# A margin on attention matmuls in the planner's list, and ten instead of nine feed-forward groups beside attention

## The chip, the cores and the metric

One core of a Trainium2 chip runs the whole program. The metric is the device time of one execution in microseconds (us). Five engines work side by side: TensorE (PE, with its weight loads as PEld), VectorE (DVE), ScalarE (ACT), GpSimd (POOL) and SyncE (SP), which here issues the DMAs. Each engine runs its own list of instructions strictly in order, so an instruction that waits holds up all that stand behind it on that engine.

## The reference, cut to what matters

Two layers over a residual stream x of 1024 tokens x 1024 features, everything in float32:

```python
for layer in range(2):
    h = rms_norm(x, mix_norm_g)
    da_q, da_k, da_v, sb_q, sb_k, sb_v, c_q, c_kv, k_r = split(h @ w_in)
    y = concat(diff_attention(...), stick_breaking(...), latent_attention(...))   # 4 heads each
    x = x + y @ w_out
    x = x + memory_attention(rms_norm(x, memx_norm_g), mem, ...)
    h = rms_norm(x, ffn_norm_g)
    x = x + square(relu(h @ w_ff1)) @ w_ff2          # hidden width 4096
```

All three attentions are causal (two of them in chunks of 64). In the stick-breaking heads a row's weights come from a running product over the keys, taken from the last key to the first.

## The kernel before

**Tiles and stages.** The 1024 tokens are 8 tiles of 128, in two halves of four tiles. A layer runs `project(0)` (the input projection of the first half), then `attention(0)` with `project(1)` beside it, `merge(0)` (output projection, memory attention, the norm ahead of the feed-forward), `attention(1)`, `merge(1)` and the feed-forward. The second half attends to all keys up to its own, so its attention is the longer one. To keep float32 accuracy an operand is split into a high and a low part, and a product is three matmuls (`mm3`, L579 to L581). Each weight block is split on the chip: DMA to `raw`, a copy on ACT (L557) and a subtraction on DVE (L558) into `w`.

**The feed-forward.** The hidden width is 16 groups of 256 columns (`NG`). A group for one half of the tokens is 48 matmuls of 512 columns in `ff1` (L579 to L581), an activation on ACT and DVE (L1249 to L1253), and 48 matmuls in `ff2` (L1272), whose result DVE adds to x (L1276). The first `G0` groups run for the first half alone, in two of the small PSUM banks, and in the list they rank behind `attention(1)` and `merge(1)`: they are what TensorE does while attention waits. The other groups then run for both halves on one split of their weights, in wide PSUM banks (tile `d`), and at the end the first `G0` groups for the second half, for which their weights are loaded and split again.

**An attention head.** Per tile of 128 queries: scores on TensorE (L1013), elementwise work on ACT, DVE and POOL, transposes on TensorE (L600), a split or copy of what they gave (L592 and L593, or L1031), the weighted sum of the values on TensorE (L1033, L1048, or L1050 and L1051), and in the 64-wide heads of the second half an addition on ACT and DVE (L1055, L1056) and one more small matmul, L1057. In a stick-breaking head (`sb_head`) the running product is a scan on DVE (L1127), followed by a multiplication on POOL (L1129). `attention(0)` runs the stick-breaking heads first, then latent, then differential ones; `attention(1)` runs stick-breaking, differential, latent.

**What sets the order.** Nothing is scheduled at run time. After the program is written down, `order_engines` makes one list for each engine: it steps through a model of the chip with a cost for every instruction (`_cost`) and a latency between engines (`_LAT`), and on an engine that comes free it takes, of the instructions that the model says are ready, the one of lowest rank. `mem.rank(r)` sets the rank of what is written after it: `attention(0)` R+10, `merge(0)` R+9, `project(1)` R+20, `attention(1)` R+40, `merge(1)` R+50, the feed-forward R+60. Where the model has an instruction ready earlier than it is on the chip, it stands too early in the list, and its engine waits there.

```python
        for y in succ[x]:
            lat = 0 if e == 5 or eng[y] == 5 else _LAT[e][eng[y]]
            avail[y] = max(avail[y], f + lat)
```

Of the kernel before, what the change touches and what calls it, by code (L numbers as in the profile page):

```python
# [30 lines left out]
C_SBQ, C_SBV, C_X = 1536, 2048, 2304  # L31
FG = 2
NG = DFF // P // FG
G0 = 9
RB = 2
LATE = (((0, 0), (1, 0), (0, 1), None, (1, 1), None, None, None, None, (2, 0), (0, 2), None, (2, 1), (1, 2), None, None, None, (0, 3), (1, 3), None, None, (2, 2), (2, 3)),
        ((0, 0), (1, 0), (0, 1), None, (2, 0), (1, 1), (0, 2), (2, 1), (1, 2), (0, 3), (2, 2), (1, 3), None, (2, 3)))
# [7 lines left out]
class Mem:  # L45
# [3 lines left out]
    def __init__(self, tc):  # L49
        self.tc = tc  # L50
        self.info = {}
        self.log = []
        self.n = 0
        self.ranks = [(0, 0, 0.0)]

    def rank(self, r, at=0.0):


        self.ranks.append((len(self.tc.nc.cur_bb.bb.instructions), r, at))

    def pool(self, st, name, side=_LEFT, space=None):
        self.n += 1
# [159 lines left out]

def order_engines(mem, tc, top):
    nc = tc.nc
    seq, prio, hold = [], [], []
    marks = mem.ranks[::-1]
    r, at = 0, 0.0
    for x, i in enumerate(nc.cur_bb.bb.instructions):
        while marks and marks[-1][0] <= x:
            _, r, at = marks.pop()  # L230
        if not type(i).__name__.startswith("BassTile"):
            seq.append(i)
            prio.append((r, x))
            hold.append(at)
    place = mem.places(top)
    acc = {}
    n = len(seq)
    preds = [set() for _ in range(n)]
    eng, cost, dmab = [0] * n, [0.0] * n, [0] * n
    regions, later = {}, []  # L240
    for x, i in enumerate(seq):
        op = type(i).__name__
        eng[x] = _ENG[str(i.engine).split(".")[-1]]
        ins = [a.bass_ap for a in i.ins if hasattr(a, "bass_ap")]
        outs = [a.bass_ap for a in i.outs if hasattr(a, "bass_ap")]
        cost[x] = _cost(i, op, ins, outs, any(place.get(a.tensor.name, " ")[0] == "ps" for a in ins))
        if op == "InstDMACopy":
            b = 4
            for s, c in outs[0].ap:
                b *= int(c)  # L250
            dmab[x] = b
        pr = preds[x]
        for w, aps in ((0, ins), (1, outs)):
            for a in aps:
                t = a.tensor
                name = t.name
                dram = "DRam" in type(t).__name__ or name not in place
                key = (name, int(a.offset), tuple((int(s), int(c)) for s, c in a.ap))
                bank = not dram and place[name][0] == "ps"
                r = regions.get(key)  # L260
                if r is None:
                    r = regions[key] = _region(a, t.shape, dram, bank)
                lst = acc.get(name)
                if lst is None:
                    lst = acc[name] = []
                hit = False
                for (y, yw, yr) in lst:
                    if (w or yw or bank) and y != x and _meet(r, yr):
                        pr.add(y)
                        hit = hit or yw  # L270
                if name in place:
                    rec = place[name][4]
                    rec["uses"].append(x)
                    if w and not hit:
                        later += [(x, o) for o in place[name][3]]
                        for o in rec["before"]:
                            if "node" not in o:
                                o["node"] = len(preds)
                                preds.append(set(o["uses"]))
                                eng.append(5)  # L280
                                cost.append(0.0)
                                dmab.append(0)
                            pr.add(o["node"])
                lst.append((x, w, r))
    for x, o in later:
        preds[x].update(y for y, _, _ in acc.get(o, ()))

    n = len(preds)
    succ = [[] for _ in range(n)]
    left = [0] * n  # L290
    for x in range(n):
        left[x] = len(preds[x])
        for y in preds[x]:
            succ[y].append(x)
    prio += [(0, 0)] * (n - len(prio))
    avail = hold + [0.0] * (n - len(hold))
    pend = [[] for _ in _ENG]
    rdy = [[] for _ in _ENG]
    free = [0.0] * len(_ENG)
    dfree = 0.0  # L300
    order = [[] for _ in _ENG]
    for x in range(n):
        if not left[x]:
            heapq.heappush(pend[eng[x]], (avail[x], x))
    done = 0
    while done < n:
        best, bt = None, None
        for e in range(len(_ENG)):
            if rdy[e]:
                t = free[e]  # L310
            elif pend[e]:
                t = max(free[e], pend[e][0][0])
            else:
                continue
            if bt is None or t < bt:
                best, bt = e, t
        e, t = best, bt
        while pend[e] and pend[e][0][0] <= t:
            a, x = heapq.heappop(pend[e])
            heapq.heappush(rdy[e], (prio[x], x))  # L320
        _, x = heapq.heappop(rdy[e])
        order[e].append(x)
        done += 1
        f = t + cost[x]
        free[e] = f
        if e == 4:
            dfree = max(dfree, f + 650) + dmab[x] / 350.0
            f = dfree + 1000
        for y in succ[x]:
            lat = 0 if e == 5 or eng[y] == 5 else _LAT[e][eng[y]]  # L330
            avail[y] = max(avail[y], f + lat)
            left[y] -= 1
            if not left[y]:
                heapq.heappush(pend[eng[y]], (avail[y], y))
    for e in range(5):
        for a, b in zip(order[e], order[e][1:]):
            tc.add_manual_dep(
                seq[b], seq[a].name,
                mybir.DependencyInfo(mybir.DependencyClass.NoSync, mybir.DependencyReason.DATA),
                reason="engine order")  # L340


def trunk(ctx: ExitStack, mem: Mem, tc: tile.TileContext, a: dict, out: bass.AP):
# [309 lines left out]
    for l in range(L):  # L653
        R = 100 * l
# [289 lines left out]
        y = {}  # L944
# [348 lines left out]


        with ExitStack() as st:
            mem.rank(R + 10)
            attention(0, Pool("at0", st=st))
        open_h(0)
        mem.rank(R + 9)
# [10 lines left out]
        close_banks()  # L1310
        open_banks()
        with ExitStack() as st:
            mem.rank(R + 40)
            attention(1, Pool("at1", st=st, side="right"))
        open_h(1)
        with ExitStack() as st:
# [10 lines left out]

        for g in range(G0):
            w1 = loads1(g)
# [20 lines left out]
        wring[0] = wide_ring  # L1350
        seq = [(g, (0, 1)) for g in range(G0, NG)] + [(g, (1,)) for g in range(G0)]
        steps = [(g, u) for g, us in seq for u in us]
        w1s, w2s, hds = {}, {}, {}

        def up(k):
            g, u = steps[k]
            key = (g, 0 if g >= G0 else 1)
            if key not in w1s:
# [7 lines left out]
        for k, (g, u) in enumerate(steps):  # L1366
            if k + 1 < len(steps):
                up(k + 1)
            ff2(w2s[g, 0 if g >= G0 else 1], u, hds.pop(k), True, None,
                l == L - 1 and k == len(steps) - 1)  # L1370
# [71 lines left out]
```

## Time and profile before

| | |
|---|---|
| median of 3 runs | 2953.82 us (2953.44 to 2956.3) |
| the profiled execution: own time, span | 2949.95 us, 2948.1 us |
| mean granted TensorE clock | 0.996 of full speed |
| busy: PE, DVE, ACT, POOL | 2865.3, 1931.2, 1397.4, 463.1 us |
| PE's share of the chain that ended last | 81% |

The span runs from the first to the last instruction; the execution's own time is 1.85 us longer. The ends of matmuls are modelled: a matmul of 512 columns is listed with about 389 ns, though a dense row of them starts one every 226 ns, so an engine listed as busy can still lose up to about 0.16 us between two matmuls.

### The profile page before, as it was taken

To read this page: it belongs to the slowest core of one execution; us is meant where nothing else is said; L and a number is where in the kernel's file an instruction comes from. 1 tells how busy PE (TensorE), PEld (TensorE's weight loads), DVE (VectorE), ACT (ScalarE), POOL (GpSimd) and SP (SyncE) were. 2 spreads that over 40 slices of the span, in tenths; PEclk is the share of its full clock that TensorE was granted. 3 is DMA by queue.
4 is the path that set the end of the run, shared out by engine and by line. 5 is a ranking of instruction groups with operands and counts; after the bars stand their busy time and mean duration, and the time that the engine had idled before them with its cause. 6 is when DMAs were issued, how large, how long until landed. Compare 5 with 4: busy or idle time off the path is not lost.

```text
span 2948.1 us, 46476 instructions
## 1 busy us (share of the span) xinstructions
PE 2865.3 (97%) x16818; PEld 2509.8 (85%) x16818; DVE 1931.2 (66%) x3716; ACT 1397.4 (47%) x3331; POOL 463.1 (16%) x556
## 2 busy tenths in 40 slices
PE   8989999899999999999999899998999999999999
PEld 7978999688898888888899789986888988888887
DVE  6878775887757544465567786768777575444555
ACT  5667555666635322133345675655666352122232
POOL 1352221421100000000013522224211000000000
PEclk9999999999999999999999999999999999999999
DMA  7766543534232111123257575444442321111232
GB/s 236 228 189 192 185 130 117 167 120 142 62 129 70 61 58 50 36 96 105 90 169 212 170 215 160 133 136 137 139 133 69 112 64 59 43 57 51 93 102 88
DMA packets 381237, 354.34 MB, mean 120 GB/s; under 512 B 27384, under 2 KB 301216, under 8 KB 381008
## 3 DMA queue, kind: packets, MB, share of 16 engines
q1 hardware_dynamic: 381008, 351.37, 38.7%
q8 instruction: 133, 2.18, 0.3%
q14 instruction: 96, 0.79, 0.1%
HBM read 290.40 MB, written 60.88 MB: 119 GB/s over the span
## 4 chain that ended last, share of the span: by engine, by line
PE 81%; DVE 7%; DMA 4%; ACT 3%; POOL 2%; issue 2%; SPq 1%; DVEq 0%; POOLq 0%; ACTq 0%
PE d L1272 17%; PE s L580 12%; PE s L581 12%; PE s L579 12%; PE s L1272 5%; PE s L600 4%; PE d L1013 3%; PE s L1033 2%; PE e L579 2%; PE e L581 2%; PE e L580 2%; PE e L1013 2%; DVE t L1127 1%; PE e L600 1%; PE s L1048 1%
## 5 line engine op out<-in xcount | busy, mean ns | idle before, releaser
L557 ACT ACTIVATE w<-raw 128x512 fp32r<-128x512 f32 (+1 forms) x688 | 420.6, 627 | 551.5 <-PE d L1272 241.8
L558 DVE TENSOR_TENSOR w<-raw,w 128x512 fp32r<-128x512 f32 (+1 forms) x688 | 466.5, 691 | 195.1 <-ACT w L557 192.8
L579 PE MATMUL s<-h,w 128*128 128x512 f32 x1120 | 442.6, 395 | 0.0
L581 PE MATMUL s<-h,w 128*128 128x512 f32 x1120 | 441.7, 394 | 0.0
L580 PE MATMUL s<-h,w 128*128 128x512 f32 x1120 | 441.0, 394 | 0.0
L1276 DVE TENSOR_TENSOR x<-d,x 128x1024 f32<-128x1024 f32 (+1 forms) x185 | 225.1, 1217 | 166.6 <-PE d L1272 166.5
L587 POOL TENSOR_TENSOR ms<-ms,mhalf 128x4 f32<-128x4 f32 (+3 forms) x144 | 147.8, 1030 | 1133.3 <-DVE ms L585 1124.7
L579 PE MATMUL s<-w,h 128*128 128x256 f32 (+1 forms) x1024 | 299.3, 296 | 4.3 <-ACT h L592 3.5
L581 PE MATMUL s<-w,h 128*128 128x256 f32 (+1 forms) x1024 | 299.3, 295 | 0.6 <-DVE h L593 0.6
L580 PE MATMUL s<-w,h 128*128 128x256 f32 (+1 forms) x1024 | 299.0, 296 | 0.2 <-DVE w L558 0.2
L1272 PE MATMUL d<-w,hid 128*128 128x512 f32 x1152 | 266.6, 389 | 0.0
L1249 ACT ACTIVATE r<-s 128x512 f32<-128x512 f32 x128 | 76.3, 596 | 391.2 <-issue 230.1
L1272 PE MATMUL s<-w,hid 128*128 128x512 f32 x864 | 250.1, 410 | 10.3 <-ACT w L557 5.1
L1251 DVE TENSOR_TENSOR r<-r 128x512 f32<-128x512 f32 x128 | 93.4, 730 | 250.0 <-ACT r L1249 249.8
L1272 PEld LDWEIGHTS d<-w,hid 128*128 128x128 f32 x1152 | 216.2, 188 | 44.8
L1272 PE MATMUL d<-w,t 128*128 128x512 f32 x1056 | 244.2, 389 | 0.0
L581 PEld LDWEIGHTS s<-h,w 128*128 128x128 f32 x1120 | 210.7, 188 | 38.7
L580 PEld LDWEIGHTS s<-h,w 128*128 128x128 f32 x1120 | 210.7, 188 | 38.5
L579 PEld LDWEIGHTS s<-h,w 128*128 128x128 f32 x1120 | 210.9, 188 | 38.0 <-ACT w L557 0.2
L1272 PEld LDWEIGHTS d<-w,t 128*128 128x128 f32 x1056 | 198.2, 188 | 41.1
L1069 POOL TENSOR_TENSOR sm<-sm,mhalf 128x1 f32<-128x1 f32 x192 | 128.9, 671 | 547.9 <-DVE sm L1068 425.3
L579 PEld LDWEIGHTS s<-w,h 128*128 128x128 f32 x1024 | 194.4, 191 | 6.4 <-ACT h L592 4.1
(338 smaller groups left out, 5997.4 us busy)
## 6 DMA issues: line engine op xcount, KB each, us to landing
raw<-in_w_ff SPq DMA_DIRECT2D x400, 256.0 KB
raw<-in_w_in SPq DMA_DIRECT2D x144, 256.0 KB
raw<-in_w_out SPq DMA_DIRECT2D x64, 256.0 KB
x<-in_x SPq DMA_DIRECT2D x16, 512.0 KB
o<-biasd SPq DMA_DIRECT2D x32, 256.0 KB
raw<-in_w_in SPq DMA_DIRECT2D x32, 208.0 KB
v<-sv SPq DMA_DIRECT2D x24, 256.0 KB
v<-mv SPq DMA_DIRECT2D x24, 256.0 KB
```

The source lines that it names most:

```text
L557: nc.scalar.activation(w[:, 0, o], raw, AF.Copy)
L558: nc.vector.tensor_tensor(w[:, 1, o], raw, f(w[:, 0, o]), op=ALU.subtract)
L579: nc.tensor.matmul(ps, sh, mh, start=start, stop=False)
L580: nc.tensor.matmul(ps, sh, ml, start=False, stop=False)
L581: nc.tensor.matmul(ps, sl, mh, start=False, stop=stop)
L587: nc.gpsimd.tensor_tensor(rs, ms, mhalf[:, :n], op=ALU.pow)
L600: nc.tensor.transpose(ps[:, k * P:(k + 1) * P], src[:, k * P:(k + 1) * P], ident)
L1013: nc.tensor.matmul(ps[:, c:c + w], sta, mov, start=first, stop=last[c // 512] == i)
L1069: nc.gpsimd.tensor_tensor(sm, sm, mhalf[:, :1], op=ALU.pow)
L1251: nc.vector.tensor_tensor(r2, r, r, op=ALU.mult)
L1272: nc.tensor.matmul(parts[e], hd[i][:, s, tt], w[:, e * 512:(e + 1) * 512], start=first, stop=last)
L1276: nc.vector.tensor_tensor(xt[t][:, cols], ps, xt[t][:, cols], op=ALU.add)
```

## The change

Two edits. The first adds a margin to `mem.rank`. For both attentions it is 300: in the planner's model a TensorE instruction of these stages counts as ready 300 ns later than before wherever what it needs comes from ACT, DVE or POOL. No instruction is added or altered by it; the lists of all engines come out in another order. The second sets `G0` to 10: one more group of the feed-forward runs for the first half in the small banks, and its weights are loaded and split a second time for the second half.

```diff
-G0 = 9
+G0 = 10
...
-    def rank(self, r, at=0.0):
+    def rank(self, r, at=0.0, late=0.0):
-        self.ranks.append((len(self.tc.nc.cur_bb.bb.instructions), r, at))
+        self.ranks.append((len(self.tc.nc.cur_bb.bb.instructions), r, at, late))
...
             lat = 0 if e == 5 or eng[y] == 5 else _LAT[e][eng[y]]
+            if eng[y] == 0 and e in (1, 2, 3):
+                lat += slack[y]
             avail[y] = max(avail[y], f + lat)
...
-            mem.rank(R + 10)
+            mem.rank(R + 10, late=300.0)
             attention(0, Pool("at0", st=st))
...
-            mem.rank(R + 40)
+            mem.rank(R + 40, late=300.0)
             attention(1, Pool("at1", st=st, side="right"))
```

Lines of the kernel function stand four lines lower in the changed file (L1057 becomes L1061, L1272 becomes L1276). Three places of the lists follow; a row is line, operation, output<-inputs with buffer numbers, shape.

TensorE, first layer, `attention(1)`, third stick-breaking head, its first tile (`s1_1518` is the bank of its weighted sum, `hid` and `s2`, `s3` belong to the feed-forward, `d0_1563` are scores of the next head). Before:

```order
L1048 MATMUL s1_1518_7437<-t4_1522_7452,v_1514_7421 128x256
L600 MATMUL s0_1530_7481<-ident_13_89,t4_1528_7473 128x128 x4
L1272 MATMUL s3_2256_10985<-w_2249_10966,hid_2241_10902 128x512 x3
L1057 MATMUL s1_1518_7437<-twin_21_102,u_1523_7456 128x64
L1013 MATMUL d0_1563_7622<-kst_1559_7608,o_1560_7613 128x256
L1013 MATMUL d0_1563_7622<-kst_1559_7608,o_1560_7613 128x384
```

The same place in the changed kernel:

```order
L1052 MATMUL s1_1518_7437<-t4_1522_7452,v_1514_7421 128x256
L604 MATMUL s0_1530_7481<-ident_13_89,t4_1528_7473 128x128 x4
L1276 MATMUL s2_2259_11016<-w_2249_10966,hid_2241_10902 128x512 x3
L1276 MATMUL s2_2259_11016<-w_2252_10975,hid_2242_10903 128x512
L1017 MATMUL d0_1563_7622<-kst_1559_7608,o_1560_7613 128x256
L1017 MATMUL d0_1563_7622<-kst_1559_7608,o_1560_7613 128x384
L1017 MATMUL d0_1563_7622<-kst_1559_7608,o_1561_7616 128x256
L1017 MATMUL d0_1563_7622<-kst_1559_7608,o_1561_7616 128x384
L1276 MATMUL s2_2259_11016<-w_2252_10975,hid_2242_10903 128x512 x2
L1276 MATMUL s3_2260_11017<-w_2249_10966,hid_2241_10902 128x512 x2
L1061 MATMUL s1_1518_7437<-twin_21_102,u_1523_7456 128x64
```

Between the last matmul of the sum and the small matmul that needs ACT's and DVE's work on it there stand now eight matmuls of the feed-forward and the next head's scores, where three stood. Over the stick-breaking part of `attention(1)`, from its first L1057 to its sixteenth, TensorE's list holds 212 feed-forward matmuls instead of 173, and DVE's list from the first scan to the sixteenth holds 18 weight splits (L558) instead of 15, and 5 each instead of 3 of L1251 and L1253.

SP, first layer, where the loads of `attention(1)` begin (`raw_2225` and `raw_2226` are the two halves of one `w_ff2` block of the first group, `w_2224`; `kst`, `o` and `v` are attention's keys, queries and values). Before:

```order
L554 DMA raw_2225_10812<-in_w_ff2 128x512
L803 DMA dv01_85_253<-t2_729_3954 128x256
L694 DMA dqk01q1_69_237<-t2_731_3960 128x4x128
L803 DMA dv01_85_253<-t2_733_3989 128x256
L803 DMA dv01_85_253<-t2_735_4017 128x256
L972 DMA kst_1415_7014<-sqk00k0_74_242 64x512 x2
...
L972 DMA kst_1660_8035<-dqk01k0_70_238 64x512 x2
L554 DMA raw_2226_10816<-in_w_ff2 128x512
L554 DMA raw_2236_10885<-in_w_ff1 128x4x128
```

In the changed kernel:

```order
L558 DMA raw_2225_10812<-in_w_ff2 128x512
L698 DMA dqk01q1_69_237<-t2_731_3960 128x4x128
L807 DMA dv01_85_253<-t2_733_3989 128x256
L807 DMA dv01_85_253<-t2_735_4017 128x256
L558 DMA raw_2226_10816<-in_w_ff2 128x512
L976 DMA kst_1415_7014<-sqk00k0_74_242 64x512 x2
L807 DMA dv01_85_253<-t2_737_4045 128x256
```

The second half of the block is now issued ahead of attention's loads; the next group's first block (`raw_2236`) stays behind them.

TensorE, first layer, the end of `merge(1)` (`h_2126` is what the feed-forward of the second half reads, `t4_2202` the last tile's norm). Before:

```order
L600 MATMUL d0_2205_10705<-ident_13_89,t4_2202_10698 128x128 x4
L600 MATMUL d1_2206_10712<-ident_13_89,t4_2202_10698 128x128 x4
L1272 MATMUL s3_2458_12181<-w_2448_12123,hid_2438_12051 128x512
L579 MATMUL s2_2468_12219<-h_1328_6625,w_2460_12199 128x512
...
L581 MATMUL s3_2471_12250<-h_1328_6625,w_2463_12208 128x512
L579 MATMUL s2_2482_12301<-h_2126_10342,w_2460_12199 128x512
```

In the changed kernel:

```order
L585 MATMUL s3_2499_12414<-h_1328_6625,w_2491_12372 128x512
L604 MATMUL d0_2205_10705<-ident_13_89,t4_2202_10698 128x128 x4
L604 MATMUL d1_2206_10712<-ident_13_89,t4_2202_10698 128x128 x4
L584 MATMUL s3_2499_12414<-h_1328_6625,w_2491_12372 128x512
...
L583 MATMUL s2_2510_12465<-h_2126_10342,w_2488_12363 128x512
```

Between the last transposes of `merge(1)` and the first matmul that reads their result there stood 49 other matmuls of 512 columns, and now there stand 11.

## Rows read from the trace of the kernel before

**Rows 1.** The page, busy time of each engine (us, share of the span, instructions).

```profile
PE 2865.3 (97%) x16818; PEld 2509.8 (85%) x16818; DVE 1931.2 (66%) x3716; ACT 1397.4 (47%) x3331; POOL 463.1 (16%) x556
```

**Rows 2.** Stretches: length, busy (count) of PE, PEld, DVE, ACT, POOL; clock; DMA; GB/s.

```profile
155.00:350.00 195.00, 182.44 (x1194) 162.91 (x1195) 155.44 (x443) 131.85 (x429) 70.16 (x97) 0.96 0.63 193
523.00:619.00 96.00, 82.07 (x442) 64.89 (x443) 83.17 (x144) 59.52 (x138) 47.59 (x42) 0.98 0.48 142
619.00:760.00 141.00, 138.27 (x864) 122.17 (x863) 106.45 (x213) 90.68 (x224) 14.77 (x22) 1.00 0.44 132
1000.00:1250.00 250.00, 250.00 (x1104) 207.04 (x1103) 113.53 (x136) 50.77 (x89) 0.00 (x0) 1.00 0.15 47
1600.00:1800.00 200.00, 184.97 (x1233) 164.75 (x1232) 157.46 (x454) 136.81 (x444) 74.74 (x102) 0.98 0.66 198
1986.00:2085.00 99.00, 84.43 (x464) 67.14 (x465) 86.03 (x149) 62.23 (x145) 48.18 (x43) 1.00 0.45 136
```

**Rows 3.** PE's waits, whole span: waiter <- releaser: us in total, times, longest.

```profile
PE s L1057 <- DVE u L1056: 12.7, 24, 1.2
PE s L600 <- DVE t L615: 8.0, 1, 8.0
PE s L1272 <- ACT w L557: 5.1, 2, 2.9
PE s L600 <- DVE t L1105: 3.5, 2, 1.8
...
PE d L1013 <- ACT t L1099: 1.0, 1, 1.0
```

**Rows 4.** Timeline, 578 to 581 us: start, us, engine, line, [idle before <- releaser].

```profile
578.01 0.28 PE L1048 MATMUL s<-t,v 128*128 128x256 f32 x1
...
578.50 2.02 DVE L1127 TENSOR_TENSOR_SCAN t<-t,zero 128x896 f32<-128x896 f32 x1
...
580.44 0.26 DVE L1056 TENSOR_TENSOR u<-s,u 64x128 f32<-64x128 f32 x1
...
580.75 0.43 PE L1057 MATMUL s<-twin,u 128*128 128x64 f32 x2 [1.11 <-DVE u L1056]
```

**Rows 5.** Timeline of SP's queue, 470 to 545 us: the issues of DMAs.

```profile
502.36 1.09 SPq L972 DMA_DIRECT2D kst<-sqk00k  x2
...
537.58 6.52 SPq L554 DMA_DIRECT2D raw<-in_w_ff  x6
```

**Rows 6.** Timeline of PE, 536 to 546 us.

```profile
541.50 0.50 PE L1272 MATMUL s<-w,hid 128*128 128x512 f32 x1 [2.90 <-ACT w L557]
```

**Rows 7.** Six stretches at half clock (columns of Rows 2): one, and their sum.

```profile
542.00:545.30 3.30, 3.08 (x9) 2.21 (x9) 3.21 (x9) 3.10 (x6) 0.88 (x2) 0.50 0.48 136
...
sum 22.80, PE 21.35 PEld 18.37 DVE 11.70 ACT 9.86 POOL 3.92; mean PE 3.56 PEld 3.06 DVE 1.95 ACT 1.64 POOL 0.65
```

**Rows 8.** DVE's groups, 523 to 619 us: busy us, mean ns | idle before.

```profile
L1127 DVE TENSOR_TENSOR_SCAN t<-t,zero 128x896 f32<-128x896 f32 (+3 forms) x14 | 27.5, 1964 | 0.2
...
L558 DVE TENSOR_TENSOR w<-raw,w 128x512 fp32r<-128x512 f32 x17 | 13.8, 824 | 5.4 <-ACT w L557 5.3
...
L1251 DVE TENSOR_TENSOR r<-r 128x512 f32<-128x512 f32 x3 | 4.6, 1521 | 0.0
...
L1253 DVE TENSOR_TENSOR hid<-r,hid 128x512 fp32r<-128x512 f32 x3 | 3.0, 996 | 0.2
```

**Rows 9.** POOL's costliest group, 523 to 619 us.

```profile
L1129 POOL TENSOR_TENSOR t<-t,t 128x895 f32<-128x895 f32 (+3 forms) x14 | 23.9, 1710 | 13.6 <-DVE t L1127 12.9 <-DVE x L1070 0.2
```

**Rows 10.** Groups by line, whole span: busy us, mean ns | idle before.

```profile
L1272 PE MATMUL s<-w,hid 128*128 128x512 f32 x864 | 250.1, 410 | 10.3 <-ACT w L557 5.1 <-DVE hid L1253 3.1 <-DVE sm L1068 1.0
...
L1251 DVE TENSOR_TENSOR r<-r 128x512 f32<-128x512 f32 x128 | 93.4, 730 | 250.0 <-ACT r L1249 249.8
...
L593 DVE TENSOR_TENSOR h<-s,h 128x512 fp32r<-128x512 f32 x64 | 41.8, 684 | 6.8 <-ACT h L592 6.8
...
L592 ACT ACTIVATE h<-s 128x512 fp32r<-128x512 f32 x64 | 35.8, 597 | 13.7 <-PE s L600 13.5
```

More of the change, by code (lines that the diff above doesn't have):

```diff
@@ L53, in __init__ @@
         self.n = 0
-        self.ranks = [(0, 0, 0.0)]
-    def rank(self, r, at=0.0):
-        self.ranks.append((len(self.tc.nc.cur_bb.bb.instructions), r, at))
+        self.ranks = [(0, 0, 0.0, 0.0)]
+    def rank(self, r, at=0.0, late=0.0):
+        self.ranks.append((len(self.tc.nc.cur_bb.bb.instructions), r, at, late))
     def pool(self, st, name, side=_LEFT, space=None):
@@ L224, in order_engines @@
     nc = tc.nc
-    seq, prio, hold = [], [], []
+    seq, prio, hold, slack = [], [], [], []
     marks = mem.ranks[::-1]
-    r, at = 0, 0.0
+    r, at, late = 0, 0.0, 0.0
     for x, i in enumerate(nc.cur_bb.bb.instructions):
         while marks and marks[-1][0] <= x:
-            _, r, at = marks.pop()
+            _, r, at, late = marks.pop()
         if not type(i).__name__.startswith("BassTile"):
@@ L234, in order_engines @@
             hold.append(at)
+            slack.append(late)
     place = mem.places(top)
```

## The prediction

> **What bounds the kernel now.** I read the page first, then stretches of the span, then who waits for whom, then single waits in order of time. TensorE is listed as busy for 2865.3 us, 97% of the span [rows 1], so what can be gained without fewer matmuls is its idle time, 2948.1 - 2865.3 = 82.8 us, and what hides under the modelled ends. The stretches say where that idle time lies [rows 2]. In the wide feed-forward (1000 to 1250 us) there is none: 1104 matmuls in 250 us, one every 0.226 us. It lies in the attentions. First layer: `attention(0)` loses 195 - 182.44 = 12.6 us, the stick-breaking part of `attention(1)` 96 - 82.07 = 13.9 us, its other heads only 2.7 us. Second layer: 15.0 us and 14.6 us in the two places of the first kind. These four stretches hold 56 of the 83 us, and both edits work on them.
>
> The waits name their sort [rows 3]. The greatest is L1057 for DVE's L1056: 24 waits, 12.7 us. Ten further groups name an attention matmul that waits for ACT or DVE, 27 waits and 20.6 us together; the first and the last of them are shown. L1272 waits twice, 5.1 us, for a weight split. The rest are DMAs of attention's operands and the start of the kernel, which the change does not aim at.
>
> One wait close up [rows 4]: the last L1048 starts at 578.01 and ends at 578.29; DVE is in a scan from 578.50 to 580.52 and does L1056 behind it; L1057 starts at 580.75, 2.46 us after the last L1048 ended, and TensorE was idle for the last 1.11 us of these. So the list has L1057 too early: the planner counted on the addition sooner than DVE, held by the scan, could do it.
>
> **The change part by part.** *The margin.* It adds no work; it puts other matmuls between what attention gives and what it needs. In the place just read, three feed-forward matmuls stood between; now eight do, and the next head's scores of 1280 columns: by the dense pace 8 x 0.226 + 1280/512 x 0.226 = 2.4 us and the four transposes besides, against the 2.46 us that the chain took. That wait should go. Over the stage there are 212 feed-forward matmuls instead of 173, 39 over 16 tiles: 39/16 x 0.226 = 0.55 us more cover for each tile, shared by the two to four waits of a tile, so 0.15 to 0.5 us for each. I take 0.25 us for each visible wait. L1057: 24 x 0.25 = 6 us (bounds 0 and 12.7). The 27 others: 27 x 0.25 = 6.75, of which I take 6, since some are shorter (bounds 0 and 20.6). Waits under the modelled ends, up to 0.389 - 0.226 = 0.16 us each, have no rows; the bounds are 0 and 51 more such waits at 0.16 = 8 us, and with nothing that favours an end I take the middle, 4 us.
>
> *SP's queue.* `raw_2226` now stands ahead of attention's loads. Before, those loads were issued from 502.36 us on, the weights behind them from 537.58 [rows 5], and TensorE stood for 2.90 us at 541.50 for that split [rows 6]; the second layer has the other wait, 5.1 us together [rows 3]. Its cause goes. Next late is the first block of the following group, still behind the same loads, which TensorE reaches some ten matmuls later. So I take half, 2.5 us (bounds 0 and 5.1).
>
> *The clock.* Six stretches, 22.8 us in all, ran at half of full speed, 1.2 instead of 2.4 GHz [rows 7], among them 542.0 to 545.3 just after that wait of 2.90 us. Each cost up to half its length. If the wait shrinks, that one may not occur: 3.3 x 0.5 = 1.7 us (bounds 0 and 11.4 for all six).
>
> *The tenth group.* Its 96 matmuls of the first half leave the wide stage and run beside attention; TensorE's work is the same. What is added is the second load and split of its weights, 8 blocks a layer, beside work that has TensorE as its bound; ACT and DVE are idle for more than half of 1000 to 1250 us [rows 2], so there it costs nothing. If that cover were gone, a layer would pay 8 x 0.824 = 6.6 us of DVE time [rows 8]. In the small banks L1272 has idle time of 10.3 us over 864 [rows 10], 0.012 us each, in the wide ones none: 96 x 0.012 = 1.1 us lost over both layers.
>
> *DVE in the stick-breaking stage.* Here the added matmuls cost something. DVE is busy for 83.17 of 96 us [rows 2], and the stage now holds 3 more L558, 2 more L1251 and 2 more L1253: 3 x 0.824 + 2 x 1.521 + 2 x 0.996 = 7.5 us [rows 8] against an idle time of 12.8 us. In exchange 39 x 0.226 = 8.8 us of matmuls move into the stage. So the stage may grow by 8.8 us at no loss, and DVE needs 7.5 of these. It fits, but fuller queues on DVE lengthen other chains; I charge 1.5 us a layer, 3 us (bounds 0 and 15).
>
> A rule speaks against this part. The row is L1251's: 1.521 us in this stage [rows 8], 0.730 us over the whole span [rows 10]; POOL is at its multiplications of 1.710 us there [rows 9]. The Trainium skill, page "SBUF — State Buffer", section "SBUF: two separate sides", says that VectorE and GpSimd share a port pair under an exclusive lock: a DVE instruction with two SBUF inputs and a GpSimd one exclude each other for the whole instruction. The row agrees in kind, since all of L558, L1251 and L1253 read two SBUF tensors and take longer here. By the row they cost 7.5 us a layer; by the rule at its worst each of the seven also sits out a whole L1129, 7 x 1.710 = 12.0 us more, and the sum would be that of the second rival below.
>
> *The tail of `merge(1)`.* Between its last transposes and their use stood 49 matmuls, 11.1 us of cover; now 11, 2.5 us. The split behind them takes about 0.6 us on ACT and 2 x 0.68 on DVE [rows 10], about 2 us. It is still hidden, with half a microsecond to spare, and I charge 0.5 us a layer, 1 us; if the chain is late by 5 us, it costs 4.5 us a layer.
>
> *Sum.* Gains 6 + 6 + 4 + 2.5 + 1.7 = 20.2; losses 1.1 + 3 + 1 = 5.1; together 15 us off the profiled execution's 2949.95. That execution is 3.9 us (0.13%) below the median of the runs, 2953.82, so the forecast is 2953.82 - 15 = about **2939 us**.
>
> **The rivals.** *The waits merely move (no change).* The margin acts on the planner's clock, not on what the planner has wrong: a scan of 1.96 us [rows 8] followed by whatever queues behind it. Longer lists between two steps also push back the next step on ACT and DVE, and the tenth group adds its own. If the visible attention waits stay and only the SP move and its clock stretch are gained, less the losses, the time is 2953.8 - 4.2 + 5.1 = 2954.7. For it: in the stick-breaking stage TensorE and DVE are both over 85% busy, so neither has much to give. Against it: the place shown gains 2 us of cover where 1.1 us was lacking.
>
> *DVE becomes the bound (slower).* If the seven added DVE instructions are each held for a whole L1129, the stage grows by 7.5 + 12.0 = 19.5 us, while 8.8 us leave the wide stage: 10.7 us a layer, 21 us. With the gains outside this stage, of some 6 in `attention(0)` and 2.5 on SP, that is 2953.8 + 21 - 8.5 = 2966. It decides as soon as DVE's added time in the stage, with what it holds up, passes 8.8 us by more than the gains elsewhere, that is from about 13 us a layer on. Against it: DVE still had 12.8 us free there.
>
> *The tail of `merge(1)` shows (no change).* At the start of the kernel, where nothing covers a norm's chain, TensorE waits 8.0 us for L615 [rows 3]. If the spare half microsecond is used up and such a chain shows whole at both merges, the 15 us are gone: 2939 + 16 = 2955.
>
> *All of it (faster by more).* If nearly all waits of attention for ACT and DVE go, hidden ones too, with half of the clock's loss: 12.7 + 12 + 6 + 5 + 5, less 5, makes 36, about 2918.
>
> **How the numbers follow.** The forecast, a gain of 7 to 25 us, has 0.55; more than that 0.10; the waits merely move 0.15; the tail shows 0.08; DVE as the bound 0.12. A measurement of this kernel can tell about 0.2%, 5.9 us, from no change. Faster by more than that: the forecast and "all of it", 0.65 and a little of what lies beside, 0.67; the same 0.20; slower 0.13. The likeliest case alone spans 2929 to 2947. For 8 in 10 the range reaches to the case of moved waits above and, below, part of the way to "all of it": 2922 to 2957.
>
> **What would show it.** Right: the four stretches named lose fewer than 56 us together, 40 to 48; the waits of L1061 (then) for DVE drop from 24 to half or less; the wait of 2.90 us for a split at the start of `attention(1)` shrinks; the stick-breaking stage gets longer by 4 to 8 us in each layer and the wide feed-forward starts later, but by less than the 21.7 us that it is shorter. Wrong: idle time in the stick-breaking stage stays at 14 us or grows, with DVE over 90% busy; a wait for the splits of `h` at the end of `merge(1)`; new waits for DMAs of attention, whose order on SP has moved too; or more stretches at half clock.

## The result and the profile after

The changed kernel takes 2938.01 us (median of 4 runs, 2936.27 to 2939.04); the kernel before, beside it, 2954.43 (4 runs). The ratio is 0.9944, 95% interval 0.9932 to 0.9956: 16.4 us faster, where 15 were forecast. Its profiled execution took 2936.27 us, with a span of 2934.5, 13.6 less than before.

The page of the changed kernel, busy time of each engine, as in [rows 1]:

```profile
PE 2859.3 (97%) x16818; PEld 2512.1 (86%) x16818; DVE 1941.6 (66%) x3740; ACT 1412.2 (48%) x3347; POOL 470.1 (16%) x556
```

TensorE's idle time is 2934.5 - 2859.3 = 75.2 us, 7.6 less than before. The other 6 us of the span are a fall of TensorE's listed busy time with as many matmuls: time that had lain under their modelled ends.

Stretches of the changed kernel (columns as in [rows 2]); the stick-breaking part of `attention(1)` is now some 4 to 8 us longer:

```profile
155.00:350.00 195.00, 181.51 (x1215) 162.96 (x1213) 155.64 (x454) 135.12 (x439) 77.20 (x104) 0.98 0.65 196
523.00:623.00 100.00, 90.83 (x490) 73.40 (x489) 88.53 (x152) 65.17 (x151) 50.38 (x42) 0.98 0.48 140
...
1600.00:1800.00 200.00, 186.63 (x1260) 168.44 (x1259) 158.53 (x459) 140.50 (x449) 80.15 (x107) 0.98 0.66 198
1986.00:2089.00 103.00, 92.63 (x505) 76.54 (x505) 86.72 (x155) 64.76 (x154) 46.59 (x40) 0.97 0.42 120
```

The reader is to see where the idle time fell. In `attention(0)` TensorE still stands 13.5 and 13.4 us (12.6 and 15.0 before). In the stick-breaking stage it stands 9.2 and 10.4 instead of 13.9 and 14.6. The four stretches lose 46.4 us instead of 56, inside the 40 to 48 that the prediction named.

TensorE's waits in the changed kernel, as in [rows 3] (lines stand four lower):

```profile
PE s L1061 <- DVE u L1060: 14.1, 16, 4.1
PE s L604 <- DVE t L619: 8.3, 1, 8.3
PE s L1052 <- DVE t L597: 5.0, 5, 1.5
...
PE d L1017 <- ACT t L1103: 3.2, 3, 1.1
```

The wait of L1272 for a weight split (5.1 us) is gone. The small matmul, now L1061, waits 16 times instead of 24, but 14.1 us instead of 12.7, and its longest wait rose from 1.2 to 4.1 us. Two of the sixteen are of another kind. The first of them, in the changed kernel's timeline from 502 to 543 us:

```profile
502.62 0.33 SPq L558 DMA_DIRECT2D raw<-in_w_ff  x1
...
536.83 6.65 SPq L558 DMA_DIRECT2D raw<-in_w_ff  x4
...
540.18 0.63 ACT L561 ACTIVATE w<-raw 128x512 fp32r<-128x512 f32 x1 [3.63 <-DMA raw<-in_w_ff]
541.34 0.63 ACT L561 ACTIVATE w<-raw 128x512 fp32r<-128x512 f32 x1 [0.53 <-DMA raw<-in_w_ff]
541.87 0.26 ACT L1059 ACTIVATE u<-s 128x128 f32<-128x128 f32 x1
542.16 0.28 DVE L1060 TENSOR_TENSOR u<-s,u 64x128 f32<-64x128 f32 x1 [3.04 <-ACT u L1059]
542.50 0.43 PE L1061 MATMUL s<-twin,u 128*128 128x64 f32 x2 [3.05 <-DVE u L1060]
```

SP issues `raw_2226` at 502.62, ahead of attention's loads. `raw_2236`, the second group's first block, stays behind them and is issued from 536.83 on. ACT, which runs its list in order, stands 3.63 us at the copy of that block; behind it in ACT's list is L1059, which has nothing to do with weights, and behind that DVE's L1060 and TensorE's L1061. The view names DVE's addition as the releaser; the cause is a DMA. The second layer has the same at 1995.20, with 4.12 us. The two are 7.17 us together; the other fourteen are 6.9.

The clock, in the half-clock stretches of the changed kernel (columns as in [rows 2]): four of them, with their sum.

```profile
543.70:547.10 3.40, 3.40 (x13) 3.03 (x13) 2.30 (x6) 0.93 (x2) 0.55 (x1) 0.50 0.62 169
...
1994.40:2001.20 6.80, 6.00 (x19) 5.23 (x20) 4.32 (x9) 3.34 (x10) 0.55 (x1) 0.50 0.38 116
sum 23.80, PE 21.58 PEld 18.38 DVE 13.05 ACT 10.36 POOL 3.58; mean PE 5.39 PEld 4.60 DVE 3.26 ACT 2.59 POOL 0.89
```

Before there were 22.8 us in six [rows 7], so nothing is seen to be gained here; the two shown begin about 1 us after the end of the long wait at 542.50, and during the one that ended at 1995.20.

### The profile page after: what moved, and what is told of

It is laid out like the page before. It is cut to its first block, busy times and chain, and to the rows that moved or that the text cites. A ratio compares the mean times of both kernels' runs of the same rounds, so it can differ in the third digit from the quotient of the medians.

```text
span 2934.5 us, 46519 instructions
## 1 busy us (share of the span) xinstructions
PE 2859.3 (97%) x16818; PEld 2512.1 (86%) x16818; DVE 1941.6 (66%) x3740; ACT 1412.2 (48%) x3347; POOL 470.1 (16%) x556
## 4 chain that ended last, share of the span: by engine, by line
PE 84%; DVE 5%; DMA 5%; ACT 2%; issue 1%; POOL 1%; SPq 1%; DVEq 0%; ACTq 0%; POOLq 0%
PE d L1276 16%; PE s L583 12%; PE s L584 12%; PE s L585 12%; PE s L1276 7%; PE s L604 4%; PE d L1017 3%; PE e L583 2%; PE e L585 2%; PE e L584 2%; PE s L1037 2%; PE e L1017 2%; PE e L604 1%; DVE t L1131 1%; PE s L1052 1%
## 5 line engine op out<-in xcount | busy, mean ns | idle before, releaser
L561 ACT ACTIVATE w<-raw 128x512 fp32r<-128x512 f32 (+1 forms) x704 | 429.3, 626 | 540.9 <-PE d L1276 232.6
L562 DVE TENSOR_TENSOR w<-raw,w 128x512 fp32r<-128x512 f32 (+1 forms) x704 | 474.3, 687 | 172.3 <-ACT w L561 169.1
L1280 DVE TENSOR_TENSOR x<-d,x 128x1024 f32<-128x1024 f32 x177 | 215.2, 1217 | 159.3 <-PE d L1276 159.3
L1276 PE MATMUL s<-w,hid 128*128 128x512 f32 x960 | 277.6, 410 | 2.2 <-DVE sm L1072 1.0
L1276 PE MATMUL d<-w,hid 128*128 128x512 f32 x1056 | 244.8, 389 | 0.0
L1276 PE MATMUL d<-w,t 128*128 128x512 f32 x1056 | 244.2, 389 | 0.0
L1276 PEld LDWEIGHTS d<-w,t 128*128 128x128 f32 x1056 | 198.2, 188 | 41.1
L1276 PEld LDWEIGHTS d<-w,hid 128*128 128x128 f32 x1056 | 198.2, 188 | 41.0
L1253 ACT ACTIVATE r<-s 128x512 f32<-128x512 f32 x128 | 76.4, 597 | 323.8 <-issue 200.0
## 6 DMA issues: line engine op xcount, KB each, us to landing
raw<-in_w_ff SPq DMA_DIRECT2D x416, 256.0 KB
raw<-in_w_in SPq DMA_DIRECT2D x144, 256.0 KB
raw<-in_w_out SPq DMA_DIRECT2D x64, 256.0 KB
o<-biasd SPq DMA_DIRECT2D x32, 256.0 KB
v<-sv SPq DMA_DIRECT2D x24, 256.0 KB
v<-mv SPq DMA_DIRECT2D x24, 256.0 KB
```

The costliest lines, as they stand in the source:

```text
L561: nc.scalar.activation(w[:, 0, o], raw, AF.Copy)
L562: nc.vector.tensor_tensor(w[:, 1, o], raw, f(w[:, 0, o]), op=ALU.subtract)
L1276: nc.tensor.matmul(parts[e], hd[i][:, s, tt], w[:, e * 512:(e + 1) * 512], start=first, stop=last)
L1280: nc.vector.tensor_tensor(xt[t][:, cols], ps, xt[t][:, cols], op=ALU.add)
```

## The experiments

Twelve kernels ran in four batches, each against the kernel before on the same chip (its medians there: 2953.01, 2953.74, 2951.42 and 2952.6 us). Ratios are to that kernel.

Readings below use one table that is worked out: the loss of a stage. Every matmul is charged the lower quartile of the start-to-start times that its line and form have in the trace of before; what a stage takes beyond the sum of these is its loss, visible idle time and lost pace together. The stick-breaking part runs here from the first scores of `attention(1)` to its last L1057 of a stick-breaking head. Both layers, us:

| stage | before | change | early_one | early_only | m_att1 | margin_only | late600_g11 |
|---|---|---|---|---|---|---|---|
| `attention(0)` | 73.5 | 70.2 | 71.2 | 70.6 | 68.1 | 71.8 | 68.6 |
| `merge(0)`, and on to `attention(1)` | 42.1 | 43.6 | 43.5 | 44.8 | 43.1 | 43.3 | 97.0 |
| stick-breaking part | 70.6 | 64.5 | 67.8 | 59.6 | 71.8 | 63.3 | 63.6 |
| other heads of `attention(1)` | 51.2 | 47.4 | 49.5 | 49.1 | 45.6 | 48.4 | 49.8 |
| `merge(1)` | 30.0 | 28.3 | 28.9 | 28.3 | 33.4 | 55.3 | 38.5 |
| on to the wide stage | 2.1 | 2.0 | 3.2 | 3.2 | 3.8 | 22.1 | 3.2 |
| sum | 269.5 | 256.0 | 264.1 | 255.6 | 265.8 | 304.2 | 320.7 |
| span | 2948.1 | 2934.5 | 2942.0 | 2934.8 | 2943.3 | 2983.4 | 3000.9 |

The sums differ from one another as the spans do, to 1.6 us. Each column is one execution, and executions of one list scatter. For `attention(0)` the lists of all engines are the same in before, early_one, early_only and m_att1, in both layers, yet their first row runs from 68.1 to 73.5; so the change's 70.2 there shows no gain. The traced execution of m_att1 is the fastest of its twelve, 7.5 us under their median. The stick-breaking part scatters less: g10_only has TensorE's list of before there and loses 71.8, margin_only has that of the change and loses 63.3.

### The two edits apart

**margin_only**, the change with nine groups:

```diff
-G0 = 10
+G0 = 9
```

> The margin of 300 with nine groups. My theory: attention's gain stays (its stretches lose as little as in the change), but the list now has the last of the nine groups 26 us of matmuls ahead of the end of merge(1) and nothing between merge(1)'s last transposes and their use, so that 3 to 10 us a layer come back as TensorE's waits on merge(1)'s norms and splits: 2944 to 2958. Rival, that the margin alone carries the result and the tenth group is incidental: 2936 to 2940.

Measured: 2985.41 us, ratio 1.0112 (1.0099 to 1.0126), far outside every expectation. Up to the end of `attention(1)` TensorE's list is that of the change, and the stages that the margin works on lose the same, to 1.6 us each; `merge(1)` and what follows lost 47 us more. TensorE's timeline there in the first layer:

```profile
952.66 1.63 PE L1276 MATMUL s<-w,hid 128*128 128x512 f32 x6
...
973.74 0.40 PE L585 MATMUL s<-h,w 128*128 128x512 f32 x1
...
1003.45 0.40 PE L585 MATMUL s<-w,t 128*128 128x512 f32 x1
1008.42 1.94 PE L604 MATMUL d<-ident,t 128*128 128x128 f32 x8 [4.58 <-DVE t L619]
1010.20 1.22 PE L583 MATMUL s<-h,w 128*128 128x512 f32 x2
...
1011.64 0.63 PE L585 MATMUL s<-h,w 128*128 128x512 f32 x1
1012.07 0.63 PE L583 MATMUL s<-h,w 128*128 128x512 f32 x1
```

and its waits over the span:

```profile
PE d L604 <- DVE t L619: 13.3, 4, 4.6
```

The last `ff2` matmuls of the nine groups start at 952.66 to 953.89 (in the change, with ten groups, the last starts at 989.07): with the margin, attention has used up most of them. The `ff1` matmuls of one more group for the first half follow, the last of them at 973.74. From there on `merge(1)` has only its own matmuls, and TensorE waits again and again; the last matmul ahead of the norm starts at 1003.45, the norm's chain on DVE and ACT follows, and TensorE stands for 4.58 us. The matmuls after it come 0.43 us apart, at half clock. From 960 to 1030 us TensorE's busy time and granted clock, in this kernel and then in the change:

```profile
960.00:1030.00 70.00, 57.51 (x257) 46.40 (x256) 32.88 (x52) 25.43 (x55) 1.66 (x3) 0.83 0.16 46
```

```profile
960.00:1030.00 70.00, 69.99 (x359) 58.89 (x358) 44.65 (x70) 29.91 (x64) 1.66 (x3) 1.00 0.22 68
```

So the margin alone pays from 973.74 on, in the second half of `merge(1)` and its tail, which was a rival of the prediction.

**g10_only**, the other half:

```diff
-            mem.rank(R + 10, late=300.0)
+            mem.rank(R + 10, late=0.0)
...
-            mem.rank(R + 40, late=300.0)
+            mem.rank(R + 40, late=0.0)
```

> Ten groups without a margin. My theory: TensorE's order beside attention is that of before, 33 us of matmuls of the first half follow merge(1), and 1.1 us is lost in the small banks: 2953 to 2957, the same as before. Rival, that the tenth group brings the gain: 2936 to 2942.

Measured: 2956.59 us, 1.0012 (1.0002 to 1.0021), as expected: the tenth group alone costs 3.6 us (0.6 to 6.2). Alone the edits give +32 and +4 us and together -16: they are not terms of a sum.

### How much margin

**m_att1**: the change with the margin on `attention(1)` alone.

```diff
-            mem.rank(R + 10, late=300.0)
+            mem.rank(R + 10)
```

> The change without the margin of attention(0); attention(1) keeps 300, ten groups. In the changed kernel attention(0) lost 1.3 and 2.0 us less than before in the two layers, attention(1) 7.4 and 2.5 us less. My theory, that the margin acts stage by stage on the waits it covers: attention(0) goes back to before and the rest stays, 2939 to 2944. Rival, that the stages' differences are what any new order gives and not the margin's: outside of that.

**late150**: the change with half the margin on both.

```diff
-            mem.rank(R + 10, late=300.0)
+            mem.rank(R + 10, late=150.0)
...
-            mem.rank(R + 40, late=300.0)
+            mem.rank(R + 40, late=150.0)
```

> The change with a margin of 150 instead of 300, ten groups; the list leaves 23 us of matmuls of the first half behind merge(1), as before. My theory (each attention wait shrinks by about what the margin adds): about half of the gain, 2943 to 2949. Rival, that the gain does not follow the margin's size: 2936 to 2940, or 2952 and more.

Measured: 2952.54 us, 0.9994 (0.9985 to 1.0003), and 2953.66 us, 1.0002 (0.9993 to 1.001). Both missed: the gain was all gone. In both lists `raw_2226` stands behind attention's loads on SP again, as before. TensorE's waits in m_att1:

```profile
PE s L1061 <- DVE u L1060: 11.0, 16, 1.7
PE s L1276 <- ACT w L561: 10.7, 2, 6.0
```

and in late150:

```profile
PE s L1276 <- ACT w L561: 10.4, 2, 5.5
```

The wait for the split, 5.1 us before, has doubled. The place in m_att1's timeline:

```profile
538.17 0.63 ACT L561 ACTIVATE w<-raw 128x512 fp32r<-128x512 f32 x1 [7.28 <-DMA raw<-in_w_ff]
538.85 0.80 PE L1276 MATMUL s<-w,hid 128*128 128x512 f32 x1 [5.96 <-ACT w L561]
```

The margin puts more feed-forward matmuls into the stage, so the block is wanted sooner: counted from the stage's first scores, the wait begins after 26.2 us instead of 28.8, and ends after about 32 in both kernels. In the change it is the margin on `attention(0)`, at 300, that moves `raw_2226` ahead on SP; whether it gains anything inside `attention(0)` itself is lost in the scatter of the table's first row.

**late600_g11**, twice the margin, with one more group as cover:

```diff
-G0 = 10
+G0 = 11
...
-            mem.rank(R + 10, late=300.0)
+            mem.rank(R + 10, late=600.0)
...
-            mem.rank(R + 40, late=300.0)
+            mem.rank(R + 40, late=600.0)
```

> A margin of 600 with eleven groups, so that the end of merge(1) is covered as in the change. My theory (waits shrink further with the margin until DVE is full): the waits of TensorE for ACT and DVE in attention fall to half of those of the change, 2924 to 2933. Rival, that the long waits come of DMAs behind attention's loads and of DVE's own queue, which no margin touches: 2935 to 2945.

Measured: 3001.56 us, 1.0152 (1.0136 to 1.0169), a bad miss. Its waits and one stretch:

```profile
PE e L604 <- DVE x L619: 12.8, 4, 4.3
...
PE s L1061 <- DVE u L1060: 7.1, 8, 1.9
```

```profile
460.00:535.00 75.00, 60.18 (x339) 52.33 (x339) 35.77 (x63) 32.18 (x75) 5.02 (x7) 0.80 0.30 87
```

The wait that the margin is about came down again in number, from sixteen to 8; but its 7.1 us are no less than the 6.9 of the fourteen in the change. The loss is in `merge(0)`, 97 us instead of 43.6: `project(1)` is the cover of both `attention(0)` and `merge(0)`, and the larger margin used it up beside the first (its last matmul starts at 485.91, 45 us ahead of the first scores of `attention(1)`; in the change 6.6 us ahead), as margin_only did with the groups.

### The weights' place on SP

**early_w**: the change, with the second group's `ff1` blocks also ranked ahead of `attention(1)`'s loads.

```diff
+            if g == 1:
+                mem.rank(R + 39)
             w1 = loads1(g)
+            if g == 1:
+                mem.rank(R + 60)
```

> The change, and the ff1 weights of the second group (raw_2236 and its like) ranked ahead of attention(1)'s loads on SP. My theory: the waits of 3.05 us (first layer) and 4.1 us (second layer) of L1061 in the changed kernel are those of ACT for these weights, and the stretches at half clock of 3.4 and 6.8 us come from them: 7 us of waits and up to 5 us of clock go, 2926 to 2932. Rival, that the wait moves on to the next thing behind the same loads: 2936 or more.

**early_w600**: the same in late600_g11.

> As late600_g11, and the second group's ff1 weights ranked ahead of attention(1)'s loads. My theory: 3 to 7 us below late600_g11, as the wait for these weights and the half clock behind it go, 2920 to 2930. Rival, that a wait for weights behind the loads comes elsewhere: the same as late600_g11.

Measured: early_w 2937.22 us, 0.9944 (0.9931 to 0.9957), the same as the change, as its rival had it; early_w600 3002.03 us, 1.017 (1.0153 to 1.0187), no better than late600_g11. The second says little: in late600_g11's list three of the second group's four `ff1` blocks already stand ahead of the loads, so only one was moved. In early_w the two long waits went:

```profile
PE s L1061 <- DVE u L1060: 8.1, 15, 1.4
```

Yet of 6.0 us of waits only 1.9 us of span came (2932.6): worked out as in the table, the stick-breaking part lost 31.0 us in the first layer (30.5 in the change) and 28.8 in the second (34.0). About 3 us more were lost in `attention(0)` and `merge(0)`, where TensorE's lists are those of the change.

**early_only**: the kernel before, no margin, nine groups; the first group's `ff2` and the second group's `ff1` blocks ahead of the loads.

```diff
+            mem.rank(R + 39 if g == 1 else R + 60)
             w1 = loads1(g)
+            mem.rank(R + 60)
...
-            ff2(loads2(g), 0, hd, False, BACK)
+            mem.rank(R + 39 if g == 0 else R + 60)
+            w2 = loads2(g)
+            mem.rank(R + 60)
+            ff2(w2, 0, hd, False, BACK)
```

> The kernel before, no margin, nine groups; only the second half of the first group's ff2 weights (raw_2226) and the second group's ff1 weights are ranked ahead of attention(1)'s loads on SP. Theory now: much of the change's gain in the stick-breaking stage of attention(1) comes of raw_2226 standing ahead of these loads: the wait of TensorE for the split (2.9 and 2.2 us) and the half clock behind it go, 2941 to 2948. Rival, that the order on SP is worth nothing without the margin: 2951 to 2956.

**early_one**: of that, the first group's `ff2` blocks alone (the second half of the diff).

> The kernel before, with no margin and nine groups, in which only the first group's ff2 blocks rank ahead of attention(1)'s loads; the second group's ff1 blocks stay behind them. SP issues raw_2226 early, as in the change, and raw_2236 late, as in both. Theory that the first block matters and the second comes too late to hurt much: as with both blocks early, 2936 to 2943, the wait of L1272 for a weight split gone. Rival, that the list only gains when both are early: 2945 to 2951, with a new wait of 2 to 4 us, in TensorE or ACT, for the split of raw_2236 a little further on, and half of the gain of both. Rival, that scatter between any two lists made the earlier result: 2950 to 2957.

Measured: early_only 2939.41 us, 0.9958 (0.9945 to 0.9972), 1.6 us below its range; early_one 2946.94 us, 0.9983 (0.9974 to 0.9992), the first rival's value. TensorE's waits in early_only:

```profile
PE s L1057 <- DVE u L1056: 9.3, 24, 0.7
...
PE s L1048 <- DVE t L593: 6.9, 8, 2.0
```

and in early_one, with the place of the longest:

```profile
PE s L1057 <- DVE u L1056: 12.2, 23, 1.0
PE s L1048 <- ACT x L1058: 8.4, 2, 4.2
```

```profile
541.76 0.63 ACT L557 ACTIVATE w<-raw 128x512 fp32r<-128x512 f32 x1 [4.61 <-DMA raw<-in_w_ff]
...
543.15 0.21 ACT L1058 ACTIVATE x<-s 128x64 f32<-128x64 f32 x1
...
543.41 0.86 PE L1048 MATMUL s<-t,v 128*128 128x256 f32 x4 [4.18 <-ACT x L1058]
```

In early_one the wait comes back at the next block, under another line: ACT stands at `raw_2236`'s copy, and an attention step queues behind it. So with no margin at all the place of `raw_2226` on SP is worth about 6 us, and that of the next group's blocks with it about 12. In the stick-breaking part early_only loses 59.6 us, as little as early_w with its margin (59.8).

**att1_early** and **late150_early**: m_att1 and late150 with the edit of early_only.

> The change without attention(0)'s margin (as m_att1, in which raw_2226 stood behind the loads again and TensorE waited 10.7 us for splits), with these weights ranked ahead. Theory: the 10.7 us go and the margin of attention(1) then shows, 2932 to 2940. Rival, that attention(0)'s margin is needed for itself: 2944 or more.

> A margin of 150 for both attentions, ten groups, these weights ranked ahead. Theory: without the wait for splits (10.4 us with 150 alone) it comes to 2935 to 2943. Rival, that 150 covers too little: 2945 to 2952.

Measured: 2949.97 us, 0.999 (0.9981 to 0.9998), a miss, and 2943.1 us, 0.9962 (0.9948 to 0.9977), 0.1 us above its range. Against late150 the early blocks gave 0.4%; against m_att1 nothing clear. In the stick-breaking part both gained, worked out as in the table: 66.8 us in att1_early against 71.8 in m_att1, and 64.5 in late150_early against 72.9 in late150. Part of att1_early's loss is a stretch of `attention(0)`, behind a wait of 1.56 us:

```profile
218.98 0.30 PE L1055 MATMUL s<-v,at 128*128 128x64 f32 x1 [1.56 <-DVE sm L1072]
```

```profile
219.00:230.00 11.00, 11.00 (x43) 10.45 (x44) 5.18 (x21) 4.63 (x20) 2.32 (x4) 0.53 0.35 98
```

The clock fell to half there, and the lists of that place are those of the kernel before: this is one execution's loss, the slowest of twelve, and not the edit's. Why the median of the twelve gained nothing either is open.

### The planner's cost of a scan

**scan_cost**: the change, with what the prediction's first rival called wrong in the planner set nearer to the chip.

```diff
+    if getattr(i, "is_tensor_tensor_scan", False):
+        return 100 + 2.15 * n
```

> The change, and the planner's cost of the scan set from 66 + 1.045 ns to 100 + 2.15 ns an element, near the traced 1.63 us for 640 and 2.29 us for 1024. If what is left of L1061's waits for DVE (7 us in 14 waits, without the two long ones) comes of the planner's too low cost of the scan, they fall to a third: 2931 to 2936. Rival, that DVE is simply full in this stage: 2936 to 2940, with the same waits under other names.

Measured: 2948.79 us, 0.9984 (0.9975 to 0.9994), slower than the change and outside both expectations. The waits that it aimed at did go. L1063 is the small matmul here (lines stand two lower still):

```profile
PE s L1063 <- DVE u L1062: 0.2, 1, 0.2
```

So with the scan's cost put right these waits go, but not the time. Its timeline shows the same wait for weights, longer:

```profile
546.02 0.63 ACT L563 ACTIVATE w<-raw 128x512 fp32r<-128x512 f32 x1 [8.86 <-DMA raw<-in_w_ff]
...
547.89 1.01 PE L1054 MATMUL s<-t,v 128*128 128x256 f32 x3 [6.37 <-DVE t L599]
```

`raw_2226` stands ahead of the loads in this list, and the next group's blocks behind them. With 13.2 us of such waits in both layers, the stick-breaking part still lost only 64.1 us, as in the change. The rest is in the first two rows of the table, 127.4 us together instead of 113.8; why is open.

## Why the prediction was right, point by point

The time was right, and so was the place (the stick-breaking stage). That the sum came so close is in part luck: of the 20.2 us of gains the rows show 14.5 (the five terms below), and the charges of 5.1 us are not to be found as losses of their own. The margin was to bring most of the gain. It removed waits as the prediction says, but the runs do not show that it brought the time: the order on SP alone, without a margin, brought more in the stick-breaking part (early_only).

- **L1057 waits, 6 us.** Right for the waits meant: 24 waits of 12.7 us became 14 of 6.9, a gain of 5.8. At the place that the prediction read closely the wait of 1.11 us is gone (the L1061 at 584.69 waits for nothing). "Half or less" of 24 was not reached, and the view's total rose, by the two waits that belong to the next term but one. The number of waits follows the margin: 23 or 24 in the four kernels without one (before, g10_only, early_one, early_only), 5 in att1_early and 14 to 16 in the other six with 150 or 300 and the old cost of the scan. The time does not follow it: early_only has 24 and gained 12 us, m_att1 has 16 and gained nothing.
- **The 27 other attention waits, 6 us.** Counted in the same way (attention's own matmuls waiting for ACT or DVE, groups of at least 1 us) there are 20 waits and 15.8 us, a gain of 4.8. m_att1 has 17 and 11.1 us, and no gain in time.
- **SP's queue, 2.5 us: the step that failed.** The prediction took the wait for the split as half gone and named the next late thing, the following group's first block. That block came as named, but not at half price: 5.1 us were removed and 7.17 returned, a loss of 2.1. The prediction looked for it at a feed-forward matmul; ACT's order carried it to L1061. It also treated the queue as a small term beside the margin. The stick-breaking part, worked out as in the table for every kernel, goes by the queue: where `raw_2226` stands behind the loads it loses 70.6 to 72.9 us, with or without a margin (before, g10_only, m_att1, late150), and where it stands ahead 59.6 to 67.8. Behind the loads, the margin gains nothing that can be measured (m_att1, late150). With the block ahead and no margin the ratio is 0.9983; margin and tenth group on top of that make 0.9944, a further 0.39% with an interval of about 0.15% either way, 11 us. That is one pair of lists: att1_early and scan_cost also have a margin, ten groups and the block ahead, and stand at 0.999 and 0.9984.
- **The clock, 1.7 us.** Nothing to be seen: 22.8 us at half clock became 23.8.
- **Hidden waits, 4 us.** The span fell by 13.6 us and visible idle time by 7.6, so 6, by subtraction; what this time was is not shown.
- **The charges.** The small banks, DVE and the tail of `merge(1)` were charged 5.1 us. The small banks' 1.1 us may be low: the tenth group alone cost 3.6 (g10_only). DVE's work was priced too high, at 7.5 us a layer: between the stretches of before and after its busy time rose by 5.4 us in the first layer and 0.7 in the second, the longer length of the stretches included. The price took three L1251 of 1.521 us, and the two views of tile `r`, of before and then of the change, show that these were two kinds:

```profile
L1251 DVE TENSOR_TENSOR r<-r x3: 665/1949/1949, 524.1 to 581.2; 128x512 f32<-128x512 f32 x3
```

```profile
L1255 DVE TENSOR_TENSOR r<-r x5: 691/698/890, 525.7 to 615.0; 128x512 f32<-128x512 f32 x5
```

The timeline of before shows what made the difference, a slow one and then the fast one:

```profile
580.85 1.77 POOL L1129 TENSOR_TENSOR t<-t,t 128x895 f32<-128x895 f32 x1
581.22 1.95 DVE L1251 TENSOR_TENSOR r<-r 128x512 f32<-128x512 f32 x1
```

```profile
567.00 0.67 DVE L1251 TENSOR_TENSOR r<-r 128x512 f32<-128x512 f32 x1
567.23 1.61 POOL L1129 TENSOR_TENSOR t<-t,t 128x639 f32<-128x639 f32 x1 [1.82 <-DVE t L1127]
```

The slow one starts 0.37 us inside an L1129 and ends 0.55 us behind it; the fast one starts ahead of one. An instruction that is not held takes 0.67 to 0.70 us, and in the change the five were hardly held (0.69 to 0.89): DVE's rival had counted the hold twice, in the mean of 1.521 and in a whole L1129 on top. The rule of the Trainium skill cited there (page "SBUF — State Buffer", section "SBUF: two separate sides", the exclusive lock) agrees with these rows.

- **The tail of `merge(1)`.** In the change no wait of TensorE stands from 960 to 1030 us, and the stage lost 1.7 us less than before. Its size without the tenth group, some 23 us a layer over `merge(1)` and what follows, is three times the 8.0 us by which the rival priced it in [rows 3]: the price was one wait, and several waits and the half clock behind them came.

Of the rivals, "the waits merely move" is half true: it holds for the weight wait, not for the fourteen. Its doubt of the planner's cost of the scan was right too: with that cost put right L1063 hardly waits (scan_cost).

**What stays open.** With both blocks early, the margin and the tenth group add 0.14% with an interval of about 0.19% either way (early_w against early_only), so whether the margin is worth anything once the weights come in time is not settled: no margin gave 0.9958, 150 gave 0.9962, 300 gave 0.9944, and `attention(1)` alone 0.999. Each of these is another list of the whole kernel, and such lists differ by some microseconds in places that no edit aims at. The corrected cost of the scan with both groups' blocks early was not run. No kernel tried is clearly faster than the change.

## What to carry to other kernels

Filler work beside a stage that waits is a stock: a margin that spends more of it must be paid for where the stock ran out (here `merge(1)` without the tenth group, `merge(0)` at 600), so a margin and its stock are tried together, never one by one. On an in-order engine a wait that moves shows up under another line's name; follow the chain back until a DMA or an idle engine stands there, and look at what is queued ahead of that DMA. Before a reordering is credited to the waits it aimed at, make its side effect alone: here one load's place in a queue, with none of the margin, gave a third of the gain, and with the next group's loads three quarters. And before a stage's time in two traces is compared, look how much it differs between two executions of one list.

## What the runs showed of the hardware

Stretches at half clock come at or right behind several of TensorE's longer waits: in the change 3.05 us of waiting and then 3.4 us at 0.50, and 4.12 us with 6.8 us at 0.50. They make a wait cost more than its own row says, since matmuls come 0.43 us apart there (margin_only, from 1011.22) instead of 0.226. In early_one the 4.18 us that ended at 543.41 are followed by this stretch:

```profile
544.00:547.40 3.40, 3.40 (x11) 2.72 (x10) 3.00 (x7) 2.18 (x5) 1.38 (x2) 0.52 0.75 229
```

In early_w, where the longest wait of that place is 1.95 us, there is none:

```profile
540.00:560.00 20.00, 16.81 (x89) 13.09 (x88) 13.98 (x24) 12.93 (x30) 9.05 (x7) 1.00 0.65 183
```

Yet in att1_early a stretch at 0.53 follows a wait of only 1.56 us. So the length of the wait is not the whole of it; TensorE's other gaps nearby differ too, and no run varied it alone.

Of DVE, L1251 took either 0.67 or 1.95 us in one and the same stage, and a mean over three of them is no price. Nor is the hold a matter of chance: in the traces of before and of the change all seventeen L558 (then L562) of 512 columns that start with 0.18 us or more of an L1129 (then L1133) still to run end 0.54 to 0.55 us behind it.
